# One address residue for the float32r operands, and 35 copies of each bias line, in an encoder of Hyena, attention and pooling layers

## Chip, cores and metric

The kernel runs on one core of a Trainium2 chip. The metric is device time in microseconds: the median of three executions is 2515.93 us (2515.85 to 2518.41). Smaller is better.

## What is computed

Four layers over one sequence of 512 positions with 1024 channels, all in float32. A layer adds a mixer and then a gated FFN of width 2816 to x. The mixers are, in order, Hyena, windowed attention, pooling, Hyena:

```python
for i in range(DEPTH):
    h = rmsnorm(x, norm_mix[i])
    y = hyena_mixer(h, ...) if i % 3 == 0 else window_attention(h, ...) if i % 3 == 1 else pool_mixer(h, ...)
    x = x + y
    x = x + swiglu(rmsnorm(x, norm_ffn[i]), ff_w_gate[i], ff_w_up[i], ff_w_down[i])
```

`swiglu` is `(silu(xn @ wg) * (xn @ wu)) @ wd`. A Hyena mixer projects h to three parts, applies a short convolution to each and two long ones (over all positions, with filters that a small network makes) with gates, and projects back. The attention adds to its logits a bias that depends on the distance of query and key and on the head: `bias = rel_table[t5_bucket(rel)]`, with keys up to 128 positions away.

## The kernel before

x lies in SBUF transposed, as eight tiles of 128 channels by 512 positions. Every large matrix product is done in float32r with both operands split in a high part and a rest: `mm3` (L199) issues three products, high x high, high x rest and rest x high, each of a 128x128 stationary operand (`ah` or `al`) with a 128x512 moving one (`bh` or `bl`), into one PSUM bank. `wload` (L176) brings a block of weights of 512 KB to `raw` (two buffers), ScalarE casts it in two halves to `hi` and VectorE subtracts for `lo` (five buffers each); a block feeds 24 products.

- The normed input of a stage is split to `ghs` and `gls` (8 x 512 columns each, kept for the whole program). Gate and up of an FFN (L271 to L282) make two tiles of the hidden layer at a time: weights `hi`/`lo` are stationary, `ghs`/`gls` move; 22 tiles x 2 matrices x 8 blocks of channels x 3 products per layer. The hidden layer is split to `hh0..21`/`hl0..21` (L294 to L297). The down projection (L300 to L311) moves those: 22 x 8 x 3 products per layer.
- A Hyena mixer calls `in_proj` 12 times (48 products each, `ghs`/`gls` moving), the filter and convolution work between them, and `out_proj` (192 products, `zh`/`zl` moving). The filter's `filter_time` (L359) multiplies the features `hh` (stationary) by `w3h`/`w3l` (moving).
- In the attention `qkv` (L770) has 288 products with the roles swapped: `hi`/`lo` move and `ghs`/`gls` are stationary. `project` (L927) has 192 with `ghs` and `ol` moving. The pooling mixer has 48 with `ghs`/`gls`.

Tiles are put into SBUF one behind the other in the order in which the code makes them, each rounded up to 32 bytes, pool by pool; a pool that is closed gives its place to the next. From that follow the start addresses, here modulo 256 bytes:

```text
operand                            before   after
ghs, gls                           128      32
hi, lo (all buffers)               224      32
hh0..21, hl0..21 in FFN 0, 2, 3    224      32
hh0..21, hl0..21 in FFN 1          32       32
zh, zl                             96       32
q, kh, kl, ol                      224      32
hh, w3h, w3l, first mixer          96       32
hh, w3h, w3l, second mixer         96       160
```

The columns of an operand begin at multiples of 512 or 2048 bytes behind its start, so a slice has the residue of its tile. In FFN 1 the tiles lie elsewhere because the pool `ahead` (L1025), made before them, holds `ss`, `bs` and eight tiles of the pooling mixer.

The bias of the attention is made in two steps. `bias_rows` (L837) is part of the side work `early`, of which one step is taken per pair of hidden tiles in FFN 0 (`next(side, None)`, L286): one product gives for each of the 16 heads a `line` of 512 values, one for each distance, and POOL's queue writes each line 128 times to DRAM (`rows`, L850 to L853). `load_bias` (L855) then reads for two heads a tile [128, 2, 384] in which partition p is the line shifted by p: it starts at P - 1 in copy 0 and goes to the next partition with a step of L - 1, that is in copy p one element earlier. After `bias_rows` the same side work makes the features of the second mixer's filters (three small products with sines, L349 to L353).

The order of instructions on each engine is set by the tile framework's scheduler from priorities (`high_priority`) and its own estimate of times. DMAs are issued from SP's queue, those of the bias from POOL's; POOL also copies `v` (L811) and adds up the filter's maxima (L397, L398).

```python
rn = self.rn[s][g][:, part]
cw0, cb0 = cw, cb
cw = self.tl(hp, [P, 3, n], "cw")
cb = self.tl(hp, [P, n], "cb")
```

These lines of `in_proj` (L586 to L589) make the scaled weights of the short convolution in two buffers each.

Of the kernel before, what the change touches and what calls it, by code (L numbers as in the profile page):

```python
# [10 lines left out]
F32 = mybir.dt.float32  # L11
# [7 lines left out]
P = 128  # L19
D = 1024  # L20
KD = D // P
L = 512
# [5 lines left out]
NB = L // P  # L28
NH = 16
# [4 lines left out]
HY_EMB = 33  # L34
FW = 64
NEG = -1e30
WB = (2, 5)
UB = 8
JOBS = [(0, 0), (0, 1), (1, 0), (0, 2), (1, 1), (0, 3), (1, 2), (1, 3)]
# [14 lines left out]
def constants():  # L54
# [36 lines left out]
    oh[buck[near], np.nonzero(near)[0]] = 1.0  # L91
    oh[32, ~near] = NEG
    c["bonehot"] = oh
# [15 lines left out]
class Kernel:  # L109
# [12 lines left out]
    def tl(self, pool, shape, tag, dt=F32, bufs=None):  # L122
        kw = {} if bufs is None else {"bufs": bufs}
        return pool.tile(shape, dt, tag=tag, name=self.nm(tag), **kw)


    def setup(self):
        ctx, tc, nc = self.ctx, self.tc, self.nc
        self.per = per = ctx.enter_context(tc.tile_pool(name="per", bufs=1))
        self.wp = ctx.enter_context(tc.tile_pool(name="wp", bufs=2))  # L130
        self.wk = ctx.enter_context(tc.tile_pool(name="wk", bufs=2))
        self.mm = ctx.enter_context(tc.tile_pool(name="mm", bufs=4, space=PSUM))
        self.aux = ctx.enter_context(tc.tile_pool(name="aux", bufs=2, space=PSUM))
        self.dr = ctx.enter_context(tc.tile_pool(name="dr", bufs=1, space=DRAM))
        self.x = [self.tl(per, [P, L], f"x{k}") for k in range(KD)]
        self.ghs = self.tl(per, [P, KD, L], "ghs", F32R)
        self.gls = self.tl(per, [P, KD, L], "gls", F32R)
        self.gh = [self.ghs[:, k] for k in range(KD)]
        self.gl = [self.gls[:, k] for k in range(KD)]
        self.ident = self.tl(per, [P, P], "ident")  # L140
        with self.tc.high_priority(offset=10000):
            make_identity(nc, self.ident)
        self.ones = self.tl(per, [P, 1], "ones")
        nc.gpsimd.memset(self.ones, 1.0)
        self.mean1 = self.tl(per, [P, 1], "mean1")
        nc.gpsimd.memset(self.mean1, 1.0 / D)
        self.root = self.tl(per, [P, 1], "root")
        with self.tc.high_priority(offset=30000):
            self.sqrt_ready(self.mean1)

# [25 lines left out]
    def wload(self, w, k0, nk, c0, ncols):  # L176

        nc = self.nc
        with self.tc.high_priority(offset=10000):
            raw = self.tl(self.wp, [P, nk, ncols], "raw", bufs=WB[0])  # L180
            nc.sync.dma_start(raw, w[k0 * P:(k0 + nk) * P, c0:c0 + ncols].rearrange("(k p) c -> p k c", p=P))
            parts = []
            step = min(nk, 512 // ncols)
            for k in range(0, nk, step):
                hi = self.tl(self.wp, [P, step, ncols], "hi", F32R, bufs=WB[1])
                lo = self.tl(self.wp, [P, step, ncols], "lo", F32R, bufs=WB[1])
                nc.scalar.copy(hi, raw[:, k:k + step])  # L187
# [39 lines left out]
    def rsqrt(self, ps, shape, pool):  # L227
        nc = self.nc
        v, s, r, q = (self.tl(pool, shape, f"rs_{c}") for c in "vsrq")
        nc.vector.tensor_scalar(v, ps, EPS, None, op0=ALU.add)  # L230
        nc.scalar.activation(s, v, AF.Sqrt)
        nc.vector.reciprocal(r, s)
        nc.vector.tensor_tensor(q, r, r, op=ALU.mult)
        nc.vector.tensor_tensor(q, q, v, op=ALU.mult)
        nc.vector.tensor_scalar(q, q, -0.5, 1.5, op0=ALU.mult, op1=ALU.add)
        nc.vector.tensor_tensor(r, r, q, op=ALU.mult)
        return r
# [327 lines left out]
    def in_proj(self, hp, s, g, part):  # L565

        nc, t = self.nc, self.t
        n = GS // P  # L570
        u = self.tl(hp, [P, R, GS] if part != 1 else [P, n, L], "u", bufs=UB)
        ps = [self.tl(self.mm, [P, L], "mm") for _ in range(n)]
        c0 = part * D + g * GS
        for k0 in (0, 4):
            ws = self.wload(t["hy_w_in"][s], k0, 4, c0, GS)
            for k in range(4):
                for e in range(n):
                    c = slice(e * P, (e + 1) * P)
                    self.mm3(ps[e], ws[k][0][:, c], ws[k][1][:, c], self.gh[k0 + k], self.gl[k0 + k],
                             k0 + k == 0, k0 + k == KD - 1)  # L580
        self.flush()
        j0 = c0 // P
        cw = self.hy_cw(s, j0, j0 + n)
        cb = self.hy_cb(s, j0, j0 + n)
        if part < 2:
            rn = self.rn[s][g][:, part]  # L586
            cw0, cb0 = cw, cb
            cw = self.tl(hp, [P, 3, n], "cw")
            cb = self.tl(hp, [P, n], "cb")  # L589
            nc.vector.tensor_tensor(cw, cw0, rn.unsqueeze(1).broadcast_to([P, 3, n]), op=ALU.mult)  # L590
            nc.vector.tensor_tensor(cb, cb0, rn, op=ALU.mult)
        taps = []
        with self.tc.high_priority(offset=7000):
            for e in range(n):
                p = self.tl(hp, [P, L + 2 * P], "p")
                last = (R - 1) * P
                bias = self.hy_bi(s, j0 + e, j0 + e + 1)
                nc.gpsimd.memset(p[:, 0:1], 0.0)
                nc.gpsimd.memset(p[:, L + 2 * P - 1:], 0.0)
                nc.scalar.activation(p[:, P:L + P], ps[e], AF.Identity, bias=bias)  # L600
                nc.scalar.activation(p[:, 1:P], ps[e][:, last:L - 1], AF.Identity, bias=bias)
                nc.scalar.activation(p[:, L + P:L + 2 * P - 1], ps[e][:, 1:P], AF.Identity, bias=bias)
                a = u[:, e] if part == 1 else self.tl(hp, [P, L], "a")
                w = lambda q: cw[:, q, e:e + 1]
                nc.scalar.activation(a, p[:, P:L + P], AF.Identity, scale=w(1), bias=cb[:, e:e + 1])
                for q in (0, 2):
                    nc.vector.scalar_tensor_tensor(a, p[:, q * P:q * P + L], w(q), a, op0=ALU.mult, op1=ALU.add)
                taps.append(a)
        if part == 1:
            return u  # L610
        self.pending = u, taps
        return u
# [224 lines left out]
    def bias_rows(self, pool):  # L837

        nc, t = self.nc, self.t
        tab = self.tl(self.per, [33, NH], "tab")  # L840
        nc.gpsimd.memset(tab[32:33], 1.0)
        nc.sync.dma_start(tab[0:32], t["rel_table"])
        oh = self.tl(pool, [33, L], "oh")
        nc.sync.dma_start(oh, t["bonehot"])
        ps = self.tl(self.mm, [P, L], "mm")
        nc.tensor.matmul(ps[0:NH], tab, oh, start=True, stop=True)
        line = self.tl(pool, [NH, L], "line")
        nc.scalar.copy(line, ps[0:NH])
        yield
        self.rows = self.dr.tile([NH, P, L], F32, tag="rows", name="rows")  # L850
        for h in range(0, NH, 4):
            nc.gpsimd.dma_start(self.rows[h:h + 4], line[h:h + 4].unsqueeze(1).broadcast_to([4, P, L]))
            yield  # L853

    def load_bias(self, ap, g, e):  # L855
        bias = self.tl(ap, [P, 2, 3 * P], "bias", bufs=3)
        h0 = 4 * g + 2 * e
        self.nc.gpsimd.dma_start(bias, bass.AP(self.rows.tensor, self.rows.offset + h0 * P * L + P - 1,
                                               [[L - 1, P], [P * L, 2], [1, 3 * P]]))
        return bias  # L860

    def scores(self, ap, g, n, e):
# [99 lines left out]

    def pool(self, ahead):
        nc, t = self.nc, self.t
        self.pool_ss = self.tl(ahead, [P, 2, NB], "ss")
        bs = self.tl(ahead, [P, KD], "bs")
        nc.vector.tensor_tensor(bs, self.pl_b, self.pl_s, op=ALU.mult)
        with self.tc.high_priority(offset=AHEAD):
            xt = [self.pool_turn(ahead, 0)]
        with self.tc.tile_pool(name="pool", bufs=2) as pp, self.tc.tile_pool(name="pool1", bufs=1) as p1:  # L970
# [9 lines left out]
            ss = self.tl(p1, [P, NB], "st")  # L980
# [105 lines left out]
```

## Time and profile before

| | before |
|---|---|
| median of three executions | 2515.93 us |
| the profiled execution | 2522.24 us |
| its span, first to last instruction | 2520.5 us |
| mean granted clock of TensorE | 0.984 |
| TensorE, products | 2424.2 us, 11062 instructions |
| VectorE / ScalarE / POOL | 1478.0 / 966.6 / 62.5 us |
| DMA queues SP / POOL | 234.17 / 7.37 MB |

The stages in the profile's time: first Hyena mixer to 378 us, FFN 0 to 781, attention to 1090, FFN 1 to 1464, pooling to 1495, FFN 2 to 1876, second Hyena mixer to 2147, FFN 3 to the end. Products are pipelined: a record of one of 512 columns lasts about 0.39 us while the next starts some 0.23 us after it, so it is the distance of starts that tells the pace, and a busy TensorE can still be slower than it might be.

### The profile page before, as it was taken

What the parts mean: (1) busy time and instruction counts of PE and PEld (TensorE: products, weight loads), DVE (VectorE), ACT (ScalarE), POOL (GpSimd) and SP (SyncE); (2) the same over time, 40 slices, a digit from 0 to 9 for tenths busy, and PEclk for the clock granted to TensorE, in tenths of its full rate; (3) what the DMA queues carried; (4) which work ended last, traced back from release to release, by engine and by line L of the source; (5) the groups of instructions that cost most, each with busy time, mean ns of one, the idle gap of its engine ahead of it and who ended that gap; (6) DMA issues with size and microseconds to landing.
All of it is one profiled execution on the core that took longest, in us unless ns stands there. A gap on an engine that the chain in (4) does not pass through costs nothing.

```text
span 2520.5 us, 29516 instructions
## 1 busy us (share of the span) xinstructions
PE 2424.2 (96%) x11062; PEld 1971.7 (78%) x11062; DVE 1478.0 (59%) x2487; ACT 966.6 (38%) x1771; POOL 62.5 (2%) x161
## 2 busy tenths in 40 slices
PE   7999989699998989999999989999989999999999
PEld 5778877487887778888888777888878888888887
DVE  7989885246334688654443354444338998544432
ACT  5543333133333567543332353333225443433321
POOL 0210000000000011000000000000000000000000
PEclk9999999799999999999999999999999999999999
DMA  4343224733333222233333223333232332333332
GB/s 149 127 158 109 76 67 97 116 92 92 92 100 105 68 93 91 84 92 92 92 94 99 88 64 92 93 97 95 93 133 84 101 101 67 92 95 98 92 94 98
DMA packets 180195, 243.42 MB, mean 97 GB/s; under 512 B 10977, under 2 KB 139633, under 8 KB 177876
## 3 DMA queue, kind: packets, MB, share of 16 engines
q1 hardware_dynamic: 174996, 234.17, 30.0%
q0 software_dynamic: 5056, 7.37, 2.2%
q8 instruction: 87, 1.43, 0.2%
q14 instruction: 56, 0.46, 0.1%
HBM read 218.41 MB, written 23.07 MB: 96 GB/s over the span
## 4 chain that ended last, share of the span: by engine, by line
PE 92%; DVE 3%; DMA 3%; ACT 2%; issue 1%; SPq 0%; ACTq 0%; DVEq 0%
PE mm L202 16%; PE mm L203 16%; PE mm L204 16%; PE aux L204 10%; PE aux L202 10%; PE aux L203 10%; PE aux L424 2%; DMA raw<-in_ff_w_gate 2%; PE aux L702 2%; PE aux L653 1%; PE aux L699 1%; PE mm L914 1%; PE aux L644 1%; PE aux L645 1%; PE mm L999 1%
## 5 line engine op out<-in xcount | busy, mean ns | idle before, releaser
L188 DVE TENSOR_TENSOR lo<-raw,hi 128x512 fp32r<-128x512 f32 x700 | 484.9, 694 | 763.3 <-ACT hi L187 756.1
L187 ACT CAST hi<-raw 128x512 fp32r<-128x512 f32 x700 | 434.2, 621 | 1095.7 <-PE mm L203 662.3
L202 PE MATMUL mm<-ghs,hi 128*128 128x512 f32 x1168 | 470.5, 405 | 28.0 <-ACT hi L187 23.8
L204 PE MATMUL mm<-ghs,lo 128*128 128x512 f32 x1168 | 468.9, 402 | 0.0
L203 PE MATMUL mm<-gls,hi 128*128 128x512 f32 x1104 | 444.8, 403 | 0.0
L202 PEld LDWEIGHTS mm<-ghs,hi 128*128 128x128 f32 x1168 | 222.4, 191 | 86.9 <-ACT hi L187 27.9
L204 PE MATMUL aux<-ghs,lo 128*128 128x512 f32 x704 | 279.5, 397 | 1.2 <-DVE lo L188 1.2
L202 PE MATMUL aux<-ghs,hi 128*128 128x512 f32 x704 | 279.4, 397 | 0.0
L203 PE MATMUL aux<-gls,hi 128*128 128x512 f32 x704 | 279.1, 396 | 0.0
L204 PEld LDWEIGHTS mm<-ghs,lo 128*128 128x128 f32 x1168 | 221.9, 190 | 53.1 <-DVE lo L188 0.5
L203 PEld LDWEIGHTS mm<-gls,hi 128*128 128x128 f32 x1104 | 210.2, 190 | 51.3 <-issue 2.1
L204 PEld LDWEIGHTS aux<-ghs,lo 128*128 128x128 f32 x704 | 132.6, 188 | 35.1 <-DVE lo L188 2.9
L203 PEld LDWEIGHTS aux<-gls,hi 128*128 128x128 f32 x704 | 132.6, 188 | 32.1
L202 PEld LDWEIGHTS aux<-ghs,hi 128*128 128x128 f32 x704 | 132.6, 188 | 32.0
L203 PE MATMUL mm<-hl,hi 128*128 128x512 f32 x352 | 137.4, 390 | 0.0
L203 PE MATMUL aux<-hl,hi 128*128 128x512 f32 x352 | 137.4, 390 | 0.0
L202 PE MATMUL mm<-hh,hi 128*128 128x512 f32 x352 | 137.3, 390 | 0.0
L202 PE MATMUL aux<-hh,hi 128*128 128x512 f32 x352 | 137.2, 390 | 0.0
L204 PE MATMUL aux<-hh,lo 128*128 128x512 f32 x352 | 136.9, 389 | 0.0
L204 PE MATMUL mm<-hh,lo 128*128 128x512 f32 x352 | 136.9, 389 | 0.0
L292 DVE TENSOR_TENSOR t<-aux,rstd 128x512 f32<-128x512 f32 x88 | 60.4, 687 | 64.0 <-PE aux L204 64.0
L296 ACT CAST hh<-t 128x512 fp32r<-128x512 f32 x88 | 54.6, 620 | 109.8 <-DVE t L293 109.8
(276 smaller groups left out, 3492.0 us busy)
## 6 DMA issues: line engine op xcount, KB each, us to landing
raw<-in_ff_w_gate SPq DMA_DIRECT2D x88, 512.0 KB
raw<-in_ff_w_up SPq DMA_DIRECT2D x88, 512.0 KB
raw<-in_ff_w_down SPq DMA_DIRECT2D x88, 512.0 KB
raw<-in_hy_w_in SPq DMA_DIRECT2D x48, 512.0 KB
kd<-k SPq DMA_DIRECT2D x32, 512.0 KB
kt<-kd SPq DMA_DIRECT2D x16, 1024.0 KB
raw<-in_hy_w_out SPq DMA_DIRECT2D x16, 512.0 KB
raw<-in_at_w_qkv SPq DMA_DIRECT2D x12, 512.0 KB
```

The source lines that it names most:

```text
L187: nc.scalar.copy(hi, raw[:, k:k + step])
L188: nc.vector.tensor_tensor(lo, raw[:, k:k + step], hi.bitcast(F32), op=ALU.subtract)
L202: mm(ps, ah, bh, start=first, stop=False)
L203: mm(ps, ah, bl, start=False, stop=False)
L204: mm(ps, al, bh, start=False, stop=last)
L292: nc.vector.tensor_tensor(t2, u[e], rstd, op=ALU.mult)
L296: nc.scalar.copy(a, t2)
L424: nc.tensor.matmul(po[:, ty, e], w, ab[:, r, e], start=m == 0, stop=m == 1)
L644: mm(ps[:, j, e], fwd[:, e, j], u[:, j], start=e == 0, stop=False)
L645: mm(ps[:, j, e], f2(e, j), u[:, 2 + j], start=False, stop=e == 1)
L653: mm(ps[:, j, e], fwd[:, e, r0 + j], u[:, r0 + j], start=e == 0, stop=e == 1)
L702: mm(y[:, e, r * P:(r + 1) * P], v[:, e * P:(e + 1) * P], w, start=st, stop=sp)
```

## The change

Small tiles (`ones`, `mean1`, `root`, and the pooling mixer's `ss` and `bs`) are made ahead of `ghs`, which moves the large tiles behind them, and `cw` and `cb` get four buffers, which moves what lies behind those in a Hyena mixer. The residues are in the table above. `rows` holds 35 copies of a line. A bias tile is read in four pieces of 32 partitions: piece a begins in copy a, 32 x a elements earlier, so that it needs copies a to a + 31.

```diff
+STEP = 32
+COPIES = P // STEP - 1 + STEP
...
         self.x = [self.tl(per, [P, L], f"x{k}") for k in range(KD)]
+        self.ones = self.tl(per, [P, 1], "ones")
+        self.mean1 = self.tl(per, [P, 1], "mean1")
+        self.root = self.tl(per, [P, 1], "root")
+        self.pool_ss = self.tl(per, [P, 2, NB], "ss")
+        self.pool_bs = self.tl(per, [P, KD], "bs")
         self.ghs = self.tl(per, [P, KD, L], "ghs", F32R)
...
-        self.ones = self.tl(per, [P, 1], "ones")
         nc.gpsimd.memset(self.ones, 1.0)
-        self.mean1 = self.tl(per, [P, 1], "mean1")
         nc.gpsimd.memset(self.mean1, 1.0 / D)
-        self.root = self.tl(per, [P, 1], "root")
...
-            cw = self.tl(hp, [P, 3, n], "cw")
-            cb = self.tl(hp, [P, n], "cb")
+            cw = self.tl(hp, [P, 3, n], "cw", bufs=4)
+            cb = self.tl(hp, [P, n], "cb", bufs=4)
...
-        self.rows = self.dr.tile([NH, P, L], F32, tag="rows", name="rows")
-        for h in range(0, NH, 4):
-            nc.gpsimd.dma_start(self.rows[h:h + 4], line[h:h + 4].unsqueeze(1).broadcast_to([4, P, L]))
-            yield
+        self.rows = self.dr.tile([NH, COPIES, L], F32, tag="rows", name="rows")
+        nc.gpsimd.dma_start(self.rows, line.unsqueeze(1).broadcast_to([NH, COPIES, L]))
+        yield
...
-        self.nc.gpsimd.dma_start(bias, bass.AP(self.rows.tensor, self.rows.offset + h0 * P * L + P - 1,
-                                               [[L - 1, P], [P * L, 2], [1, 3 * P]]))
+        for a in range(P // STEP):
+            o = self.rows.offset + (h0 * COPIES + a) * L + P - 1 - a * STEP
+            self.nc.gpsimd.dma_start(bias[a * STEP:(a + 1) * STEP],
+                                     bass.AP(self.rows.tensor, o, [[L - 1, STEP], [COPIES * L, 2], [1, 3 * P]]))
...
-        self.pool_ss = self.tl(ahead, [P, 2, NB], "ss")
-        bs = self.tl(ahead, [P, KD], "bs")
+        bs = self.pool_bs
```

On POOL's queue, from the write of the lines in FFN 0 to the copies of v at the end of `qkv` in the attention, before:

```order
L852 DMA rows<-line_3252 512x1x512 x4
L734 MEMSET kl_1074_5531 64x1024
L734 MEMSET kl_1075_5532 64x1024
L858 DMA bias_5547<-rows 128x2x384
L858 DMA bias_5549<-rows 128x2x384
L811 COPY v_5524<-q_1119_5747 128x256
L811 COPY v_5524<-q_1121_5752 128x256
L811 COPY v_5524<-q_1123_5757 128x256
L858 DMA bias_6184<-rows 128x2x384
L811 COPY v_5524<-q_1125_5762 128x256
```

and in the changed kernel:

```order
L855 DMA rows<-line_3254 560x1x512
L738 MEMSET kl_1076_5530 64x1024
L738 MEMSET kl_1077_5531 64x1024
L863 DMA bias_5546<-rows 32x2x384 x4
L863 DMA bias_5551<-rows 32x2x384 x4
L863 DMA bias_6189<-rows 32x2x384 x4
L815 COPY v_5523<-q_1121_5752 128x256
L815 COPY v_5523<-q_1123_5757 128x256
L815 COPY v_5523<-q_1125_5762 128x256
L815 COPY v_5523<-q_1127_5767 128x256
```

The write is one DMA in place of four, a bias tile takes four issues, and the third tile's issues stand ahead of all copies of v.

Further on in the attention the loads stand between the additions for the filters of the second mixer (mx), before:

```order
L858 DMA bias_6781<-rows 128x2x384
L397 TENSOR_TENSOR mx_7139<-mx_7139,k_1490_7143 128x512
L858 DMA bias_7271<-rows 128x2x384
L398 TENSOR_TENSOR mx_7139<-mx_7139 128x256
L397 TENSOR_TENSOR mx_7384<-mx_7384,k_1563_7388 128x512
L398 TENSOR_TENSOR mx_7384<-mx_7384 128x256
```

and in the changed kernel:

```order
L863 DMA bias_6795<-rows 32x2x384 x4
L401 TENSOR_TENSOR mx_7156<-mx_7156,k_1492_7160 128x512
L863 DMA bias_7288<-rows 32x2x384
L402 TENSOR_TENSOR mx_7156<-mx_7156 128x256
L863 DMA bias_7288<-rows 32x2x384 x3
L401 TENSOR_TENSOR mx_7407<-mx_7407,k_1565_7411 128x512
L402 TENSOR_TENSOR mx_7407<-mx_7407 128x256
```

The second of these tiles is issued in part ahead of one addition (now L402) and in part behind it.

On VectorE, in the first Hyena mixer, the scaled convolution weights of a later input projection (cw, cb) between the filter's work, before:

```order
L590 TENSOR_TENSOR cw_1375<-vec_93,rn_34_165 128x6
L591 TENSOR_TENSOR cb_1376<-vec_93,rn_34_165 128x2
L440 TENSOR_TENSOR k_225_940<-aux_931,e_224_937 128x512
L441 TENSOR_TENSOR k_225_940<-aux_931,e_224_937 128x512
L384 TENSOR_TENSOR ab_1068<-aux_1069,dec_1055 128x2x512
```

and in the changed kernel:

```order
L594 TENSOR_TENSOR cw_1377<-vec_95,rn_36_167 128x6
L595 TENSOR_TENSOR cb_1378<-vec_95,rn_36_167 128x2
L594 TENSOR_TENSOR cw_1706<-vec_95,rn_37_168 128x6
L595 TENSOR_TENSOR cb_1707<-vec_95,rn_37_168 128x2
L444 TENSOR_TENSOR k_227_942<-aux_933,e_226_939 128x512
L445 TENSOR_TENSOR k_227_942<-aux_933,e_226_939 128x512
L388 TENSOR_TENSOR ab_1070<-aux_1071,dec_1057 128x2x512
```

A second pair stands right behind the first; before, it came 31 rows later.

## Rows read from the trace of the kernel before

**Rows 1.** the page, busy time by engine, and the shares of the chain that ended last

```profile
PE 2424.2 (96%) x11062; PEld 1971.7 (78%) x11062; DVE 1478.0 (59%) x2487; ACT 966.6 (38%) x1771; POOL 62.5 (2%) x161
...
PE 92%; DVE 3%; DMA 3%; ACT 2%; issue 1%; SPq 0%; ACTq 0%; DVEq 0%
```

**Rows 2.** windows of TensorE over runs of one kind of product: us, then as headed

```profile
core 0: us, PE busy (x), PEclk, DMA share, GB/s
...
1117.32:1339.42 222.10, 222.10 (x949) 1.00 0.32 93
...
660.91:780.37 119.46, 119.46 (x528) 1.00 0.31 97
...
1408.09:1463.95 55.86, 55.86 (x245) 1.00 0.30 94
...
2109.09:2126.99 17.90, 17.90 (x79) 1.00 0.35 118
823.25:842.38 19.13, 19.13 (x83) 1.00 0.27 82
1045.57:1089.92 44.35, 44.35 (x192) 1.00 0.28 89
```

**Rows 3.** timeline of TensorE, filter products of the first mixer: start us, us, what

```profile
92.75 0.40 PE L382 MATMUL aux<-w3h,hh 128*128 128x512 f32 x1
...
93.67 0.40 PE L202 MATMUL mm<-ghs,hi 128*128 128x512 f32 x1
```

**Rows 4.** the same windows of TensorE, before the hole in FFN 0 and in it

```profile
427.00:448.50 21.50, 21.50 (x93) 1.00 0.82 91
448.50:486.00 37.50, 13.73 (x40) 0.64 0.89 117
```

**Rows 5.** timeline of SP, POOL and ScalarE around it; landing of the writes of rows

```profile
430.50 6.00 SPq L181 DMA_DIRECT2D raw<-in_ff_w_gate  x2
...
427.19 4.51 POOL L852 DMA_DIRECT2D rows<-line  x4 [124.44 <-ACT line L848]
...
468.54 0.62 ACT L187 CAST hi<-raw 128x512 fp32r<-128x512 f32 x1 [33.17 <-DMA raw<-in_ff_w_gate]
...
DMA to landing us min/median/max: 3.5/5.8/50.7
```

**Rows 6.** DMA queues from 435 to 468 us: packets, MB, share of 16 engines

```profile
q0 software_dynamic: 787, 3.21, 95.0%
q1 hardware_dynamic: 582, 0.58, 5.0%
```

**Rows 7.** windows of all engines in the two Hyena mixers

```profile
core 0: us, PE busy (x) PEld busy (x) DVE busy (x) ACT busy (x) POOL busy (x), PEclk, DMA share, GB/s
...
150.00:240.00 90.00, 90.00 (x443) 75.31 (x442) 81.82 (x122) 31.13 (x58) 2.79 (x14) 1.00 0.38 135
...
1990.00:2096.00 106.00, 106.00 (x507) 87.60 (x506) 103.83 (x154) 45.05 (x85) 1.32 (x20) 1.00 0.28 92
```

**Rows 8.** issues of bias and rows on POOL (ns), and lines of VectorE

```profile
L858 POOL DMA_DIRECT2D bias<-rows x8: 708/712/747, 782.8 to 996.8; - x8
...
  DVE den L890: 16.9, 2
  DVE m L880: 12.9, 1
...
L852 POOL DMA_DIRECT2D rows<-line x4: 1080/1096/1259, 427.2 to 430.6; - x4
...
L880 DVE CUSTOM_DVE_ANT_0 lg<-mm,bias,vec 128x256 f32<-128x256 f32 (+1 forms) x64 | 34.3, 544 | 15.1 <-PE mm L878 14.8
...
L590 DVE TENSOR_TENSOR cw<-vec,rn 128x6 f32<-128x6 f32 x16 | 4.7, 295 | 0.0
```

**Rows 9.** timeline at the start: start us, us, what

```profile
3.25 0.20 ACT L173 ACTIVATE vec<-vec 128x1 f32<-128x1 f32 x1 [1.02 <-DMA vec<-in_vec]
...
6.05 0.69 DVE L221 TENSOR_TENSOR ssq<-ssq,sq 128x512 f32<-128x512 f32 x1 [6.05 <-ACT sq L220]
```

## The prediction

> **What bounds the kernel now.** I read the page first: TensorE is busy for 96% of the span and the chain that ended last is TensorE for 92% [rows 1]. So the question is how fast products follow each other, and where TensorE stands still.
>
> For the first I took windows over unbroken runs of one kind of float32r product [rows 2]. A window's x counts each product that touches it, so between the first start and the last lie x less 1 spacings (less 2 in the window at 2109, into which an earlier product runs). All these products are 128x128 by 512, at the full clock (2.4 GHz, granted 1.00), with nothing waited for:
> - gate and up, FFN 1: 222.10 / 948 = 234.3 ns. Moving ghs/gls at residue 128, stationary hi/lo at 224.
> - down, FFN 0: 119.46 / 527 = 226.7 ns. hh/hl at 224, hi/lo at 224.
> - down, FFN 1: 55.86 / 244 = 228.9 ns. The same lines, but hh/hl at 32, since the tiles of "ahead" lie ahead of them.
> - output projection of the second Hyena mixer: 17.90 / 77 = 232.5 ns. zh/zl at 96, hi/lo at 224.
> - qkv: 19.13 / 82 = 233.3 ns. Here the roles are swapped, hi/lo move (224) and ghs/gls are stationary (128).
> - output projection of the attention: 44.35 / 191 = 232.2 ns, where one moving operand in three is at 224 and the rest at 128.
>
> FFN 0 and FFN 1 run the same code with the same shapes in the down projection; what differs is an address, and the spacing goes from 226.7 to 228.9. The swapped case shows that 224 for the moving operand is not enough (233.3 with 224 against 128). So what I read here is the distance between the residues of the two operands: 0 costs nothing, 64 costs 2.2 ns, 128 costs 5.8, 96 and 160 cost 6.6 to 7.6.
>
> One place has equal residues other than 224: the filter's products of w3h/w3l with hh, all at 96 in the first Hyena mixer. They come four at a time between others; from the first start, 92.75, to that of the fifth product, 93.67, lie four spacings [rows 3]: 230 ns each, neither clearly 227 nor as dear as unequal pairs, and too short a run to settle it.
>
> For the second I looked for holes in TensorE. The largest is in FFN 0: 40 products in the 37.5 us from 448.5, against 93 in the 21.5 us before [rows 4]. What ended it is a load of ff_w_gate, issued at 430.50, whose first half ScalarE could split only at 468.54 [rows 5]. Between lie the four writes of the bias lines to DRAM, issued from 427.19, the slowest landing after 50.7 us [rows 5]. From 435 to 468 their queue moved 3.21 MB (97 GB/s) and took 95% of the DMA engines, the weights' queue moved 0.58 MB [rows 6].
>
> **The change, part by part.**
>
> *(a) One residue.* After the change ghs, gls, hi, lo, every hh/hl, zh/zl, q, kh, kl and ol start at residue 32, and the second mixer's hh, w3h, w3l at 160. If equal residues are what counts, every spacing becomes 226.7 ns:
> - gate and up: 4 layers x 22 tiles x 2 x 8 x 3 = 4224 products, with the pooling mixer's 48 of the same operands 4272, x 7.6 ns = 32.5 us. TensorE never waits in these stages, and the down projections already take 24 products per 512 KB load at 226.7 ns, so loads and splits keep up. I take 32, because a few of FFN 0 run at the low clock behind the hole.
> - down, FFN 1: 528 x 2.2 ns = 1.2 us. The other three: nothing.
> - Hyena: 24 input projections x 48 = 1152 x 7.6 = 8.8 us, and 384 of the output projections x 5.8 = 2.2 us: 11 us if TensorE alone were the limit. It isn't: in 1990 to 2096 VectorE is busy for 103.8 of 106 us, in 150 to 240 for 81.8 of 90 [rows 7]. Between 0 and 11; I take 6.
> - attention: qkv 288 x 6.6 = 1.9 us, output 192 x 5.5 = 1.1 us; some falls into waits of TensorE on other engines there. Between 0 and 3; I take 2.5.
>
> Together 42 us, between 33 and 48.
>
> *(b) 35 copies in place of 128.* The write shrinks from 4.19 to 16 x 35 x 2 KB = 1.15 MB; at the rate of rows 6 it takes 12 us, not 43. It is issued at the same point, behind the copy of "line", so it is over near 441. The load of 430.50 must have landed by about 447.2 (cast 0.62 us and subtraction 0.69 us before TensorE runs dry at 448.55). In the burst it gets about 18 GB/s (0.58 MB in 33 us), some 0.2 MB, and the other 0.3 MB at the 96 GB/s at which loads run elsewhere [rows 2] needs 3 us: landed near 444. The hole then is gone. Its price is 37.5 - 40 x 0.234 = 28.1 us [rows 4]; I take 27, and for the range 14 to 28, since the write by one DMA from 16 partitions may run slower than by four from 4 each.
>
> *(c) Bias loads in four pieces.* 32 issues on POOL for 8. An issue took 0.71 us for 256 runs of 1.5 KB and 1.10 us for 512 lines [rows 8], so one of 64 runs costs between 0.3 and 0.71 us, and a tile at most 4 x 0.71 = 2.8 us for 0.71. Behind them on POOL stand the copies of v and the filter's additions (L397, L398), for which the filter's norm waits; three places, at most 2.1 us each. But POOL stood idle before these loads (16.9 us before two of them, 12.9 us before one, waiting for VectorE to free the tile), and the scores never wait for a bias tile: what VectorE waits for at L880 is TensorE (14.8 us of 15.1) [rows 8]. Cost 0, at worst 6 us.
>
> *(d) Rest.* The scale tiles cw and cb get 4 buffers, which lets their 16 operations each (cw 0.30 us on average [rows 8], cb shorter) stand earlier on VectorE: 0, within 2 us. The sum for the pool's bias now stands first on VectorE and waits for "vec", which ScalarE used at 3.25 us, while VectorE's first other work comes at 6.05 [rows 9]: 0. With three steps fewer in FFN 0's side work the filter's features come 288 products earlier, in the same stage: 0.
>
> Sum: 42 + 27 = 69 us. Against the profiled execution (2522.24 us, span 2520.5) that is 2453; it lies 6.3 us above the median of 2515.93, so I forecast 2447 us.
>
> **A rule against it.** The Trainium skill, page "TensorE: Matmul & The Clock Gate", section "Step-by-step: what each phase is for", says that TensorE has two independent read ports and that "Loading the next tile's weights doesn't steal SBUF read bandwidth from the running matmul." By that rule addresses have no price, the sum would be (b) alone, and the first rival below would come true. The trace speaks against it: 226.7 and 228.9 ns for the same code [rows 2].
>
> **The rivals.**
>
> *Addresses have no price.* The spacings then belong to the stages: gate and up fill two accumulators at a time, down four. For it: the 234.3 ns are found in gate and up alone. Against: the two down projections. Then only (b) is left: 2516 - 27 = 2489. Chance 0.06.
>
> *The moving operand's own residue has a price besides.* With 32 for all, every spacing would be FFN 1's 228.9: gate and up gain 4272 x 5.4 = 23 us, three down projections lose 1584 x 2.2 = 3.5, Hyena and attention give some 6: 25.5 + 27, so 2463. For it: rows 3 read 230 at equal residues. Against: the swapped roles. Chance 0.13.
>
> *The write still starves the weights.* If the single DMA runs at half the rate, it ends near 453, and the load lands near 454: a hole of some 7 us, and with the low clock behind it only 13 to 18 of the 28 us come back: 2456 to 2461. Chance 0.12.
>
> *Slower: prices of both operands add up.* If each operand pays for its distance from 224 by itself, the stationary at 32 pays too, which no row shows. The worst sum in rows 2 is 7.6 + 6.6, a spacing of 241. Gate and up then lose 4272 x 6.6 = 28 us, the down projections 1584 x 14.2 + 528 x 12 = 29, the rest about 14; with (b) 2516 + 71 - 27 = 2560. It decides from a common spacing of about 236: there the 28 us of the hole are eaten up. Against: rows 3, where both operands at 96 would read 238 or more and read 230. Chance 0.03.
>
> The change doing what it says is no question: the addresses follow from the order in which tiles are made.
>
> **How the numbers follow.** The forecast has 0.66: 2440 (everything in (a), all of the hole) to 2459 (33 of (a), 24 of the hole). The range reaches to the second and third rival and takes in a few us for moved instructions: 2438 to 2470. It leaves out the first and the last rival. A measurement of this kernel can tell about 0.2%, 5 us, from no change. Faster 0.95; same 0.02 (a spacing near 236, or starving with the first rival); slower 0.03.
>
> **What would show it.** Gate and up at 226.7 ns, as FFN 0's down projection is now; FFN 1's down projection at 226.7; no hole in FFN 0; the write landing within some 15 us; Hyena windows with VectorE close to full. Wrong would be: down projections that get slower, or 234 in gate and up unchanged.

## The result, and the profile after

The changed kernel takes 2447.3 us, median of four executions (2446.41 to 2448.21). The kernel before, run beside it, takes 2517.17 us (2515.85 to 2518.87). The ratio is 0.9722, 95% interval 0.9705 to 0.9739: 69.9 us less. Forecast were 2447 us, between 2438 and 2470.

The page of the changed kernel, busy time, queues and the chain that ended last:

```profile
PE 2374.2 (97%) x11062; PEld 1959.8 (80%) x11062; DVE 1476.1 (60%) x2487; ACT 966.0 (40%) x1771; POOL 69.6 (3%) x182
...
q1 hardware_dynamic: 174996, 234.17, 31.1%
q0 software_dynamic: 1840, 4.29, 1.0%
...
PE 92%; DVE 3%; ACT 2%; issue 1%; DMA 0%; SPq 0%; ACTq 0%; DVEq 0%
```

Against [rows 1] TensorE has the same 11062 products in 50 us less of busy time; DMA has gone from 3% of the chain to nothing. POOL's queue moves 4.29 MB in place of 7.37.

Windows of TensorE over the same kinds of products as in [rows 2], in the same order, and as the last two the stretch in which the hole was:

```profile
core 0: us, PE busy (x), PEclk, DMA share, GB/s
1068.49:1283.44 214.95, 214.95 (x950) 1.00 0.33 96
622.15:741.61 119.46, 119.46 (x529) 1.00 0.32 97
1351.51:1406.86 55.35, 55.35 (x245) 1.00 0.31 95
2059.95:2079.24 19.29, 19.29 (x87) 1.00 0.28 82
780.07:796.44 16.37, 16.37 (x74) 1.00 0.33 96
998.53:1041.85 43.32, 43.32 (x192) 1.00 0.30 91
424.00:437.50 13.50, 13.50 (x62) 1.00 0.90 120
437.50:480.00 42.50, 42.50 (x186) 1.00 0.39 113
```

As before, x less 1 is the number of spacings, or x less 2 where an earlier product runs into the window (the first, second, fourth and fifth row):

| products | before, ns | after, ns |
|---|---|---|
| gate and up, FFN 1 | 234.3 | 214.95 / 948 = 226.7 |
| down, FFN 0 | 226.7 | 119.46 / 527 = 226.7 |
| down, FFN 1 | 228.9 | 55.35 / 244 = 226.8 |
| zh/zl, second Hyena mixer | 232.5 | 19.29 / 85 = 226.9 |
| qkv | 233.3 | 16.37 / 72 = 227.4 |
| output of the attention | 232.2 | 43.32 / 191 = 226.8 |

All kinds now have the pace that the down projection of FFN 0 had. Where a distance is named below, it is the start of the moving operand less that of the stationary one, modulo 256 bytes; the addresses are worked out from the order of the tiles, no trace shows them. In the last two windows TensorE is busy throughout at the full clock (1.00); [rows 4] showed 13.73 us of 37.5 at 0.64 there.

The timeline of the changed kernel around the write of `rows`: start us, us, engine, what.

```profile
426.66 5.81 SPq L185 DMA_DIRECT2D raw<-in_ff_w_gate  x2
...
423.39 0.81 POOL L855 DMA_DIRECT2D rows<-line  x1 [122.11 <-ACT line L852]
...
438.51 0.62 ACT L191 CAST hi<-raw 128x512 fp32r<-128x512 f32 x1 [7.17 <-DMA raw<-in_ff_w_gate]
```

And the tile `rows`: issues in ns, then landing of its DMAs, of which the longest is the write:

```profile
L863 POOL DMA_DIRECT2D bias<-rows x32: 533/533/560, 744.0 to 951.4; - x32
L855 POOL DMA_DIRECT2D rows<-line x1: 807/807/807, 423.4 to 423.4; - x1
...
DMA to landing us min/median/max: 2.2/3.7/13.6
```

The write lands after 13.6 us, at 437.0, and the load that in [rows 5] was split 38 us after its issue is split 11.9 us after it. ScalarE still waits 7.17 us for it, but TensorE does not. The DMA queues of the changed kernel from 427 to 436 us (one line), then from 436 to 438.5:

```profile
q0 software_dynamic: 219, 0.89, 94.7%
...
q1 hardware_dynamic: 848, 0.85, 97.0%
q0 software_dynamic: 27, 0.02, 5.0%
```

Up to 436 us, with the write nearly through, the loads get no packet at all; then 0.85 MB of them come in 2.5 us.

Where the time came from, by stage, as the distance of the same products in the two profiled executions:

| stage | before | after | difference |
|---|---|---|---|
| start and first Hyena mixer | 377.8 | 375.4 | -2.5 |
| FFN 0, gate and up | 283.1 | 246.8 | -36.3 |
| attention, qkv | 85.0 | 78.0 | -7.0 |
| attention, scores to output | 224.3 | 222.0 | -2.3 |
| gate and up, FFN 1, 2, 3 | 3 x 249.7 | 3 x 241.8 | -23.7 |
| FFN 1, down | 124.3 | 123.2 | -1.1 |
| second Hyena mixer | 271.5 | 268.8 | -2.8 |

They sum to 75.7 us (each is rounded by itself). The profiled execution of before (2522.24 us) was 5 us above its median, that of after (2446.56 us) lies at its own, so some 6 us of these differences belong to that one execution.

### The profile page after: what moved, and what is told of

Its sections match the earlier page's. It is cut to its first block, busy times and chain, and to the rows that moved or that the text cites. A ratio compares the mean times of both kernels' runs of the same rounds, so it can differ in the third digit from the quotient of the medians.

```text
span 2444.8 us, 29542 instructions
## 1 busy us (share of the span) xinstructions
PE 2374.2 (97%) x11062; PEld 1959.8 (80%) x11062; DVE 1476.1 (60%) x2487; ACT 966.0 (40%) x1771; POOL 69.6 (3%) x182
## 3 DMA queue, kind: packets, MB, share of 16 engines
q0 software_dynamic: 1840, 4.29, 1.0%
## 4 chain that ended last, share of the span: by engine, by line
PE 92%; DVE 3%; ACT 2%; issue 1%; DMA 0%; SPq 0%; ACTq 0%; DVEq 0%
PE mm L206 16%; PE mm L207 16%; PE mm L208 16%; PE aux L208 10%; PE aux L206 10%; PE aux L207 10%; PE aux L428 2%; PE aux L706 2%; PE aux L703 1%; PE aux L657 1%; PE mm L919 1%; PE aux L648 1%; PE aux L649 1%; PE mm L1003 1%; PE aux L438 1%
## 5 line engine op out<-in xcount | busy, mean ns | idle before, releaser
L206 PE MATMUL mm<-ghs,hi 128*128 128x512 f32 x1168 | 460.7, 397 | 4.2 <-ACT ghs L515 4.2
L208 PE MATMUL mm<-ghs,lo 128*128 128x512 f32 x1168 | 459.1, 393 | 0.0
L207 PE MATMUL mm<-gls,hi 128*128 128x512 f32 x1104 | 435.6, 395 | 0.0
L208 PE MATMUL aux<-ghs,lo 128*128 128x512 f32 x704 | 274.3, 390 | 1.1 <-DVE lo L192 1.1
L206 PE MATMUL aux<-ghs,hi 128*128 128x512 f32 x704 | 274.3, 390 | 0.0
L207 PE MATMUL aux<-gls,hi 128*128 128x512 f32 x704 | 273.9, 389 | 0.0
```

The source lines that it names most:

```text
L206: mm(ps, ah, bh, start=first, stop=False)
L207: mm(ps, ah, bl, start=False, stop=False)
L208: mm(ps, al, bh, start=False, stop=last)
```

## The experiments

Nine kernels, all timed beside the kernel before; each computes the whole result. "By profile" is the distance of stages in profiled executions, as in the table above.

**1. The residue alone.** The changed kernel with the four writes of 128 copies and the bias tiles read in one DMA each, as before.

```diff
-        self.rows = self.dr.tile([NH, COPIES, L], F32, tag="rows", name="rows")
-        nc.gpsimd.dma_start(self.rows, line.unsqueeze(1).broadcast_to([NH, COPIES, L]))
+        self.rows = self.dr.tile([NH, P, L], F32, tag="rows", name="rows")
+        for h in range(0, NH, 4):
+            nc.gpsimd.dma_start(self.rows[h:h + 4], line[h:h + 4].unsqueeze(1).broadcast_to([4, P, L]))
+            yield
...
-        for a in range(P // STEP):
...
+        self.nc.gpsimd.dma_start(bias, bass.AP(self.rows.tensor, self.rows.offset + h0 * P * L + P - 1,
+                                               [[L - 1, P], [P * L, 2], [1, 3 * P]]))
```

Expected: 

> The changed kernel with the old bias path: 128 copies of each line, written by four DMAs, and each bias tile read by one. My theory (distance of the residues, and the hole as a term of its own): gate and up stay at 226.7 to 226.8 ns, the hole in FFN 0 is back with two waits of some 20 and 4 us and products at the low clock behind them, so 28 us above the changed kernel's 2447: 2475. Rival (the hole was mostly a matter of pace, so that faster products alone move it): 2447 to 2460. If instead the bias path carried more than the hole: above 2480.

Measured: 2477.31 us, ratio 0.9844 (0.983 to 0.9859), 39.5 us less than before. By profile, against the changed kernel: FFN 0's gate and up take 273.7 us in place of 246.8, so the hole is worth 26.9; qkv 80.9 in place of 78.0; all else within 0.7. The timeline of this kernel, ScalarE at the hole and TensorE in qkv:

```profile
464.44 0.62 ACT L191 CAST hi<-raw 128x512 fp32r<-128x512 f32 x1 [33.31 <-DMA raw<-in_ff_w_gate]
...
797.77 0.50 PE L206 MATMUL mm<-hi,ghs 128*128 128x512 f32 x1 [1.29 <-ACT q L803]
...
803.62 0.41 PE L825 MATMUL aux<-ident,qh 128*128 128x128 f32 x2 [1.28 <-issue]
```

The first line is the hole again. The other two are waits in qkv that the changed kernel doesn't have; see 3 and the waits in qkv behind 8.

**2. The copies alone.** The kernel before with the new `rows` and the new `load_bias`, and its old addresses (the diff is the other half of the change's).

Expected: 

> The kernel before with the new bias path alone: 35 copies by one DMA, tiles read in four pieces, addresses as before. My theory: gate and up at 234.3 ns as before, no hole in FFN 0, 28 us below before: 2489 (before 2517). Rival (pace and hole hang together): a hole of over 5 us stays, 2495 to 2510. The start of the attention was 5 us shorter after the change than the pace of its products explains; if the bias path did that, it is found here and 2484 comes out, if the pace did, it is found in the run of the residue alone.

Measured: 2486.84 us, ratio 0.9881 (0.9865 to 0.9898), 29.9 us less than before. Against the profile of before: FFN 0's gate and up 283.1 to 254.5 (-28.6), qkv 85.0 to 80.7 (-4.3), the spacings as in [rows 2]. The two halves add up: 39.5 + 29.9 = 69.4, and the whole gave 69.9.

**3. Four pieces, 128 copies.** The changed kernel with one number changed; the order of instructions is the same on every engine.

```diff
-COPIES = P // STEP - 1 + STEP
+COPIES = P
```

Expected: 

> The changed kernel with 128 copies in place of 35; the order of instructions is the same on every engine, the bias tiles are still read in four pieces. The write in the changed kernel took 13.6 us for 1.15 MB, so 4.19 MB takes some 50 us and ends near 473. Theory (the write starves the load until it ends, whatever the number of DMAs it is issued as): TensorE runs dry near 444 as in e1_residue_alone, the first split of the next load stands 30 us late, a hole of 28 us (as there) to 36 us (if nothing lands before the write's end): 2475 to 2483. Rival (four DMAs of four partitions each were the trouble, one DMA of sixteen leaves the weights their share): no hole, 2447. On the start of the attention: if reading the tiles in pieces is what shortened the qkv stage, it takes 78.0 us here as in the changed kernel; if the smaller write did, 80.9 as in e1_residue_alone.

Measured: 2471.95 us, ratio 0.9819 (0.9805 to 0.9834). The timeline of this kernel, TensorE, ScalarE and then the write on POOL:

```profile
466.91 0.80 PE L206 MATMUL mm<-ghs,hi 128*128 128x512 f32 x1 [21.25 <-ACT hi L191]
...
466.24 0.62 ACT L191 CAST hi<-raw 128x512 fp32r<-128x512 f32 x1 [33.69 <-DMA raw<-in_ff_w_gate]
...
424.59 1.17 POOL L855 DMA_DIRECT2D rows<-line  x1 [122.91 <-ACT line L852]
```

and the landings of the tile `rows`, the longest being the write's:

```profile
DMA to landing us min/median/max: 2.2/3.4/45.4
```

So one DMA of 4.19 MB starves the load as four did: 24.4 us in FFN 0 by profile, somewhat below the 28 to 36 expected, since the write was faster (92 GB/s) than its small brother (84) and the load landed some 4 us before the write's end (split at 466.24, the end at 424.59 + 45.4 = 470.0). The queues of this kernel from 428 to 442 us (the load was issued at 427.86), then from 444 to 464:

```profile
q0 software_dynamic: 336, 1.38, 95.1%
...
q0 software_dynamic: 475, 1.95, 94.2%
q1 hardware_dynamic: 475, 0.48, 6.8%
```

The load gets nothing for its first 14 us, then one packet for each of the write's, 0.48 MB in 20 us: 24 GB/s, at which its 0.52 MB are there before the write has ended. What holds its packets back for the first 14 us isn't shown.

The qkv stage takes 78.0 us, so it isn't the smaller write that shortened it. Experiment 1 differs from this one in the reading in pieces and in the number of DMAs that write the lines; nothing here tries the two apart.

**4. 70 copies.** The same with twice 35.

```diff
-COPIES = P // STEP - 1 + STEP
+COPIES = 2 * (P // STEP - 1 + STEP)
```

Expected: 

> The changed kernel with 70 copies of a line, twice 35; the order of instructions is the same. In the changed kernel the write landed 13.6 us after its issue at 423.4 and the waiting load was cast 1.5 us after that; without the weights TensorE would have run dry near 444. Theory (the load waits until the write has ended): 27 us of write, end near 451, first split near 452, TensorE back near 453.5: 9 us dry and 2 to 4 us for the low clock behind it, 2458 to 2461. Rival (the load trickles in through the burst at 18 GB/s and needs only 0.5 MB, so it lands soon after 444): a hole of 0 to 3 us, 2447 to 2450. By the first, the break-even lies near 18 us of write, some 47 copies.

Measured: 2456.15 us, ratio 0.9758 (0.9744 to 0.9773), 8.9 us above the changed kernel. Its timeline, TensorE and then ScalarE; the write was issued at 423.03:

```profile
450.61 0.80 PE L206 MATMUL mm<-ghs,hi 128*128 128x512 f32 x1 [6.51 <-ACT hi L191]
...
449.94 0.62 ACT L191 CAST hi<-raw 128x512 fp32r<-128x512 f32 x1 [18.95 <-DMA raw<-in_ff_w_gate]
```

and the landings of `rows`:

```profile
DMA to landing us min/median/max: 2.3/3.5/25.5
```

The write ends at 448.5, the load is split 1.4 us later, and 6.5 us of TensorE are lost, 8.2 by profile with the first products behind, which run at a granted clock of 0.50. In the changed kernel the interval from the write's end to the split is 1.5 us. The rival, by which the load trickles in soon after 444, falls (at its own 18 GB/s, 0.52 MB would have taken 29 us from the issue at 426.30). The theory holds here, but not as a rule: in experiment 3 the load was there before the write's end. Here too the load got its first packet 14 us after its issue, at 440.6, and then as many as the write (94 each from 442 to 446); 0.25 MB of it was in by 448, and the rest came as the write ended. The cost came out 2 us below the lower bound since the write took 25.5 us and not 27. TensorE is back 2.1 us after the write's end and was dry from 450.61 - 6.51 = 444.1; so by estimate a write that ends by 442.0, within 19 us, costs nothing, some 50 copies.

**5. ghs and gls apart.** A pad of 96 bytes behind them: they stay at 32, all that lies behind moves to 128. The order of instructions is the same.

```diff
+        self.tl(per, [P, 24], "pad")
         self.ident = self.tl(per, [P, P], "ident")
```

Expected: 

> The changed kernel with everything behind ghs/gls moved by 96 bytes: ghs/gls stay at 32, all other float32r operands lie at 128; the order of instructions is unchanged. The distance between ghs/gls and hi/lo is that of the kernel before, at other addresses. My theory: gate and up back at 234.3 ns, qkv at 233, the down projections and zh/zl at 226.7 to 227: 42 us less 1 (FFN 1) less 2 (zh) = 39 us above 2447 if all of it counts, 33 of them in the FFNs: 2480 to 2486. Rival (own residues): the stationary at 128 costs 6.6 ns everywhere, the down projections too: 2500 or more.

Measured: 2485.24 us, ratio 0.9878 (0.9863 to 0.9893): 37.9 us above the changed kernel by nothing but 96 bytes. Gate and up of FFN 1 in this kernel:

```profile
1081.55:1303.65 222.10, 222.10 (x949) 1.00 0.30 93
```

222.10 / 948 = 234.3 ns, to the digit the row of [rows 2]. The down projections, with hh/hl and hi/lo all at 128, keep 226.7. By profile each gate and up loses 7.9 us, the Hyena mixers 2.2 and 2.7, qkv 2.3, the output of the attention 1.0.

**6. All at 128.** The pad of 96 bytes ahead of ghs in place of behind gls, so that all operands stand at 128 (the second mixer's w3h, w3l and hh at 0).

Expected: 

> The changed kernel with a pad of 96 bytes ahead of ghs, so that all float32r operands stand at residue 128 in place of 32 (the second mixer's w3h, w3l and hh at 0). If only the distance of the two operands counts: 226.7 ns everywhere and 2447, within 2. If 32 itself is a good residue, or 128 a bad one (the residue that ghs and gls had before): up to 7 ns on 10400 products more, 2450 to 2520.

Measured: 2446.87 us, ratio 0.9721 (0.9706 to 0.9735), the same as the changed kernel. Gate and up of FFN 1:

```profile
1068.36:1283.30 214.94, 214.94 (x950) 1.00 0.33 96
```

At 32 and 128, and at 224 in the down projection of [rows 2], the residue itself has no price; only the distance has.

**7. What distance costs what.** The changed kernel with a pad tile ahead of hh/hl in each FFN, so that the four down projections move operands 32, 96, 192 and 224 bytes away from hi/lo; then, in a second kernel, 64, 160, 128 and 64 bytes. The order is the same in both.

```diff
             hh, hl = [], []
+            self.tl(fp, [P, (8, 24, 48, 56)[i]], "pad", bufs=1)
```

(16, 40, 32, 16 in the second.) Expected of the first: 

> The changed kernel with a small unused tile ahead of hh/hl in each FFN, so that these (moving) stand 32, 96, 192 and 224 bytes past the residue 32 of hi/lo in FFN 0, 1, 2 and 3; the order of all instructions is unchanged. My theory (only the distance counts): the down projections run at 227 to 234 ns: about 233 in FFN 1 (the distance of qkv before), and 32, 192 and 224 apart somewhere between 226.7 and 234; gate and up stay at 226.7; in all 5 to 16 us above 2447, about 2456. Rival (a moving operand has its own good residues, 224 and 32): FFN 2, whose hh/hl then lie at 224, runs at 226.7, FFN 1 at 128 is the slowest. If a distance is quicker than none, a down projection falls below 226.7 ns.

Expected of the second: 

> The changed kernel with a pad tile ahead of hh/hl, so that the down projections of FFN 0, 1, 2 and 3 move operands at distances of 64, 160, 128 and 64 from hi/lo at residue 32; the order of instructions is the same. These are the distances that e4_distances left out. If the distance alone sets the pace, as read from the kernel before: FFN 0 and 3 at 228.9 ns, FFN 1 at 234.2, FFN 2 at 232.5; 528 x (2.2 + 7.5 + 5.8 + 2.2) = 9 us, 2456. If 64 was cheap in the kernel before only because of the two residues there (moving 32, stationary 224) and any unequal pair costs 6.7 ns: all four at 233.3, 14 us, 2461.

Measured: 2460.86 us (ratio 0.9778, 0.9764 to 0.9793) and 2458.48 us (0.9768, 0.9751 to 0.9784). Windows over the four down projections of the first (of FFN 1 the unbroken part):

```profile
core 0: us, PE busy (x), PEclk, DMA share, GB/s
623.05:746.02 122.97, 122.97 (x529) 1.00 0.29 94
1357.89:1414.58 56.69, 56.69 (x244) 1.00 0.29 92
1699.30:1822.27 122.97, 122.97 (x529) 1.00 0.30 94
2332.93:2455.90 122.97, 122.97 (x528) 1.00 0.30 92
```

and of the second:

```profile
core 0: us, PE busy (x), PEclk, DMA share, GB/s
623.02:743.66 120.64, 120.64 (x529) 1.00 0.29 96
1357.53:1414.46 56.93, 56.93 (x245) 1.00 0.29 92
1699.23:1822.20 122.97, 122.97 (x529) 1.00 0.28 94
2332.90:2453.54 120.64, 120.64 (x528) 1.00 0.29 94
```

With 527 spacings in a full row and 243 in FFN 1's: 233.3 ns at distances 32, 96, 192, 224 and 128 (the first reading, 232.5, was a little low), 234.3 at 160 and 228.9 at 64. In the first kernel FFN 2 has hh/hl at residue 224, where the kernel before had its quick down projection; against hi/lo at 32 it is slow. In the second, 64 comes out at 228.9 twice, with other residues than those of [rows 2]. So the distance alone sets the pace. The first kernel's 4 x 527 x 6.6 ns = 13.9 us account for the 13.6 by which it lies above the changed one; of the second's 11.2 the down projections lose 9.7 by profile, and the rest is within the scatter of the first mixer and of qkv there (1.5 us each). Since every distance that is a multiple of 32 has now been run, no better choice than 0 is left.

**8. Two buffers.** The changed kernel with `cw` and `cb` in two buffers again, and a pad tile of the size of the other two, so that all addresses stay.

```diff
-            cw = self.tl(hp, [P, 3, n], "cw", bufs=4)
-            cb = self.tl(hp, [P, n], "cb", bufs=4)
+            cw = self.tl(hp, [P, 3, n], "cw")
+            cb = self.tl(hp, [P, n], "cb")
+            if not hasattr(self, "pad_%d" % s):
+                setattr(self, "pad_%d" % s, self.tl(hp, [P, 32], "pad", bufs=1))
```

Expected: 

> The changed kernel with cw and cb in two buffers again and a pad tile of the same size, so that every address of a float32r operand stays. If these buffers serve the addresses alone, as argued, both Hyena mixers keep their times (351.4 and 268.8 us) within 0.5 us: 2447, within 2. If the earlier scaling on VectorE is part of what the mixers gained (2.7 and 2.8 us), they give back 1 to 3 us each: 2449 to 2453.

Measured: 2446.53 us, ratio 0.9719 (0.9703 to 0.9735), the same as the changed kernel. The first mixer took 352.3 us in place of 351.4, the second 267.8 in place of 268.8: both are outside the 0.5 us expected, but in opposite directions and within the scatter of single profiles given under (a) below. So in time the buffers do nothing but place what lies behind them, though they change the order on TensorE, ScalarE, VectorE and SP's queue.

**The waits in qkv.** They are in the kernel before (1.29 and 1.23 us of TensorE, at 813.41 and 819.26) and in experiment 1, whose bias tiles come by one DMA each, and not in the changed kernel or in experiments 2, 3 and 4, which read in pieces. The timeline of ScalarE, in experiment 1:

```profile
793.85 0.62 ACT L191 CAST hi<-raw 128x512 fp32r<-128x512 f32 x1 [2.11 <-PE mm L208]
796.51 0.62 ACT L191 CAST hi<-raw 128x512 fp32r<-128x512 f32 x1 [2.04 <-PE mm L208]
797.04 1.26 ACT L803 ACTIVATE q<-mm,rs_r 128x512 f32<-128x512 f32 x2
```

and in the changed kernel, where the product that waits at 797.77 in experiment 1 starts at 769.64:

```profile
767.18 0.62 ACT L191 CAST hi<-raw 128x512 fp32r<-128x512 f32 x1 [2.11 <-PE mm L208]
767.80 0.69 ACT L803 ACTIVATE q<-mm,rs_r 128x512 f32<-128x512 f32 x1
...
768.85 1.25 ACT L803 ACTIVATE q<-mm,rs_r 128x512 f32<-128x512 f32 x2
769.99 0.61 ACT L191 CAST hi<-raw 128x512 fp32r<-128x512 f32 x1
```

In the first, a cast that waits for TensorE (2.04 us, for a buffer of `hi`) stands ahead of the q that TensorE waits for to have its PSUM bank; in the second three q stand ahead of the cast at 769.99, which waits for nothing. TensorE's own order differs too: the product `aux<-ident,qh` (L825), which waits at 803.62 in experiment 1, stands nine products later in the changed kernel. All kernels that read in pieces and write by one DMA have the second order, the kernel before and experiment 1 the first. So with the new bias path the scheduler orders both engines in another way; that it is this order that brings the 2.9 us, and not the loads themselves, is read from the traces and was not tried apart.

## Why the prediction was right, point by point

**(a) One residue: 42 us forecast, 40 measured.** Of the parts, gate and up with the pooling mixer were taken at 32: FFN 0 gave 36.3 - 28.6 (its hole, by experiment 2) = 7.7, the others 23.7 and pooling nothing, together 31.4. Down in FFN 1: 1.2 forecast, 1.1 measured. Hyena: 6 taken, measured less. In single profiles the mixers scatter by over 1 us, so I take means: from its first product with ghs the first takes 352.3 us (351.4 to 353.0) in the eight kernels whose ghs and hi share a residue, and 354.1 in the three where they don't, the second 268.9 (267.8 to 270.4) and 271.6: 1.8 + 2.7 = 4.5. That VectorE holds them back, as argued from [rows 7], fits the busy shares but was not tried apart; in the same window of the first mixer it is nearly as busy as before, though TensorE is quicker:

```profile
core 0: us, PE busy (x) PEld busy (x) DVE busy (x) ACT busy (x) POOL busy (x), PEclk, DMA share, GB/s
150.00:240.00 90.00, 89.91 (x444) 75.37 (x443) 82.05 (x122) 32.01 (x58) 2.78 (x14) 1.00 0.38 135
```

444 products there against 443: next to nothing of the 7 ns per product arrives in this stretch. Attention: 2.5 taken; 288 x (233.3 - 227.4) = 1.7 in qkv and 1.0 in the output, 2.7. The sum of the parts is 39.7, and experiment 1 gave 39.5 by medians. The reading of the distance from five rows, that 0 is the only quick one, held, and four kernels with pads ran at the pace of the distance worked out for them.

**(b) 35 copies: 27 forecast, 26.9 measured** (experiment 1 against the changed kernel; 28.6 in experiment 2 against the profile of before, and 24.4 in experiment 3, where only the number of copies differs). The write was forecast at 12 us and landed after 13.6; the load was to land 17 us after the issue of the write and was split 15 us after it. The step of the trickle was wrong: 0.2 MB was to arrive during the burst at 18 GB/s and 0.3 MB behind it at 96 GB/s, in 3 us. In the changed kernel nothing arrived during the burst, and behind it loads came at 0.85 MB in 2.5 us, some 340 GB/s. The two errors offset each other, which is luck; with a write of 25.5 us the late start of the load costs 8 us.

**(c) Bias in four pieces: 0 forecast, a gain of 2.9 measured with the new path.** This is the term that failed, with the reservation that the pieces and the single write were not tried apart. An issue takes 0.533 us, inside the bounds of 0.3 to 0.71, and as said no other engine waits for it (POOL itself does once, 2.6 us). But I looked only for what the added issues could delay. The qkv stage lost two waits of TensorE, by the traces because the scheduler put the work of ScalarE and TensorE there in another order; I compared the order on POOL and VectorE, and not on those two.

**(d) The rest: 0 forecast, and 0 for cw and cb in experiment 8.** The other small moves were not tried apart; the sum leaves nothing for them.

Together 39.7 + 26.9 + 2.9 = 69.5, against 69.9 by medians and 69 forecast. That the number agrees to the microsecond is partly luck: Hyena was taken 1.5 us too high and the pieces 2.9 too low.

**The rivals.** *Addresses have no price*: the changed kernel would have come out as experiment 2 did, 2486.84; it is 39.5 us quicker. By the rule of the Trainium skill that was weighed there, page "TensorE: Matmul & The Clock Gate", section "Step-by-step: what each phase is for", experiment 5 would have run like the changed kernel; the trace disagrees, with 234.3 ns for 226.7. The runs show the price and that it hangs on the distance, not which reads collide. *The moving operand's own residue*: refuted by experiment 6 (226.7 ns with all at 128) and by FFN 2 in experiment 7 (233.3 with 224). *The write still starves*: not with 35 copies, at 84 GB/s, but a slower write would have cost what it said: experiment 4 had 25.5 us of write and took 2456.15, which is where that rival stood. *Slower, prices add*: the stationary operand at 32 costs nothing.

The profiled execution of before lies above its median. Of the 7.0 us that went from its qkv stage, 1.7 and 2.9 are named above. Its traces show 1.6 more at the start of the stage, ScalarE and then TensorE:

```profile
791.34 0.62 ACT L187 CAST hi<-raw 128x512 fp32r<-128x512 f32 x1 [1.60 <-DMA raw<-in_at_w_qkv]
...
793.73 1.44 PE L224 MATMUL aux<-mean,ssq 128*128 128x1 f32 x6 [4.42 <-DVE ssq L221]
```

A load for qkv landed 1.6 us too late for ScalarE, which also makes the squares for ssq; TensorE waits 4.42 us for ssq there and 2.79 in the changed kernel. Why that load landed late stays open, and whether it does so in other executions.

## What to carry to other kernels

Where TensorE is the bound with float32r products, compare the distance of starts over unbroken runs of the same shape in different stages: 226.7 against 233 to 234 ns for the same product was the whole sign, busy shares hid it, and it cost a few small tiles made earlier. A write on one queue is priced by what waits on the other: give it no more time than the loaded blocks cover (here some 19 us). What lies beyond is lost in the main: with 128 copies the write took 26 us more than that, and TensorE stood still for 21. And an edit to DMAs that nobody waits for can still reorder an engine through the scheduler, so compare the order on every engine, not only on those that the edit touches.

## What was not expected of the hardware

- The price of a distance is nearly a step: 6.6 ns (233.3 - 226.7) at 32, 96, 128, 192 and 224, 7.6 at 160, but only 2.2 at 64. Behind the same mean stand different patterns of single spacings: 229 and 238 in turn at 128, 231, 231 and 238 at 96, 226, 229 and 231 at 64. What makes them isn't settled.
- Next to the four writes of 2 KB lines, the weights' queue got 15% of the bytes: 0.58 MB against 3.21 [rows 6]. Next to one write, a load issued behind it got no packet for 14 us (experiments 3 and 4). A packet of the write is 3.21 MB / 787 = 4.1 KB by the profile's count, one of the loads 0.58 MB / 582 = 1.0 KB. The Trainium skill, page "DMA: Bandwidth & Descriptors", section "Queues, rings and completion order", says that an engine takes turns between queues by whole packets; the counts in rows 6 (787 to 582) are nearer to equal than the bytes (5.5 to 1), and in experiment 3, once the load has begun, they are equal (475 and 475), which agrees with that. The 14 us without a packet are not explained by it.
